# A hybrid decoder layer on one core: products stored early are written into PSUM, the opening norms move, factors load further ahead

## The chip, the core and the metric

The kernel runs on one core of one Trainium2 chip. The metric is the device time of one execution in microseconds (us). TensorE (PE) does matrix products into PSUM; VectorE (DVE) and ScalarE (ACT) work on SBUF and PSUM; GpSimd (POOL) and SyncE (SP) mostly start DMAs here. Each engine runs its own instructions in the order they were written out for it, and an instruction that waits on a semaphore holds up all that stand behind it on that engine. The same is true of the DMA starts on the SP, ACT and POOL queues.

The order on each engine is not written by hand. A planner works from the program's order, in which every instruction gets a priority by its place; a block marked `high_priority(offset=n)` is treated as if it stood n instructions earlier. `self.lead` is 300, `self.urgent` is 1000. The order is fixed when the program is built.

## The reference, cut to what matters

One decoder layer over 1024 tokens of width 1024 (float32): a SwiGLU half-step, a mixer (recurrence, sliding-window attention, attention into a memory of 256 tokens, merged by gates), a second SwiGLU half-step.

```python
def rms_norm(x, g):
    y = xf * lax.rsqrt(jnp.mean(xf * xf, axis=-1, keepdims=True) + NORM_EPS)
    return (y * g.astype(jnp.float32)).astype(x.dtype)

def swiglu(u, w_in, w_out):
    gate, up = jnp.split(u @ w_in, 2, axis=-1)
    return (jax.nn.silu(gate) * up) @ w_out

f1 = swiglu(rms_norm(h, ffn1_pre_g[l]), ffn1_w_in[l], ffn1_w_out[l])
h = h + HALF_STEP * rms_norm(f1, ffn1_post_g[l])
...
mem_n = rms_norm(mem, mem_norm_g[l])
km, vm = jnp.split(mem_n @ w_kv, 2, axis=-1)
...
f2 = swiglu(rms_norm(h, ffn2_pre_g[l]), ffn2_w_in[l], ffn2_w_out[l])
h = h + HALF_STEP * rms_norm(f2, ffn2_post_g[l])
```

## The kernel before, in words

Activations lie with features on the 128 partitions and tokens along the free dimension, in two halves of 512 tokens (h0, h1). A weight block of 128 by 512 is loaded as a "raw" on SP's queue (`raw`, L136), cast by ACT to a high part `w_hi` (L154) and subtracted by DVE to a low part `w_lo` (L156); a product is then three matmuls per block of 128 (high by high, high by low, low by high, L247 to L249), so `product` (L257) is 12 matmuls and `project` 24 for each half of the tokens. Up to eight such weight operands are prepared ahead (`OPS`), and up to four raws.

**The first half-step's input** (`ffn_in`, L480) multiplies by Winograd's variant of Strassen's scheme: seven products in place of eight, over the quarters x11, x21 (h0) and x12, x22 (h1). For each of 22 column blocks the gate part needs only b11 and b21, which are x11 and x21 after the norm; the rest needs factors that mix both halves of the tokens. The gate part of the first 16 blocks (`FIRST`; 14 in the second half-step) is done ahead. Its first product `m` and the finished gate `g` are stored to DRAM (`first_d`, on POOL's queue) and loaded again by `ffn_in_pair` (L515), which does the remaining five products of such a "rest" block (60 matmuls). The other blocks, "pairs", do all seven products in one go.

- **Opening** (`unscaled_gates`, L411): the first `UNSCALED` = 6 gate blocks are multiplied before the norm's factor is known, with x times the gain split into high and low parts. The sum of squares of h0 goes through PE (`rstd`, L268: 8 small matmuls, some 13 small DVE instructions, 4 small matmuls that spread the result), with blocks 2 and 3 multiplied between. Blocks 0 to 3 are scaled on DVE (L439, L440), h0 is normed (`factors_norm`, L358, 8 DVE instructions), split (`factors_first`, L360: 8 casts on ACT, 8 subtractions on DVE at L304), and blocks 4 and 5 are scaled as they leave PSUM (L426). Then blocks 6 and 7 are multiplied with the normed h0 (`gates_ahead`, L475). The norm of h1 has blocks 8 and 9 between; `factors_part` and `factors_end` then make the mixed factors, and blocks 10 to 15 follow.
- **A rest block** (L515): the stored `m1` is added by DVE to two results as they leave PSUM (L533) and a third time at the end (L564). Pair blocks do the same two evictions as ACT copies (L535). The bank `px` takes the products with t2, t3 and t4 in turn; `pz` those with t1 and b22. `up` (L546) must have read `px` before the product with t4 may write on.

PSUM has eight banks of 128 by 512: four for tiles tagged "mm" (`px`, `py`, `po`, `pq`, `pgate` and others) and four for "bg" (`pz`, `pu`, the small norm results).

**The half-step's output** (`ffn_outs`, L615) runs seven phases of 11 steps; a step is 48 matmuls onto four banks. In each step a weight operand and a "hidden" factor from DRAM are used. `out_hidden` (L581) loads the factor on SP's queue into `hid` (3 buffers), casts on ACT (L303) and subtracts on DVE (L304) into two of the 32 `u` tiles; `out_next` (L590) keeps `OUT_AHEAD` = 6 of them written ahead in the program, with priority `lead`. In the first half-step the order of phases is a11, s1, s2, s3, s4, a22, a12. Phase s2 adds onto a11's banks; ACT then copies these four banks (L611, `urgent`) and s3 adds onto the same banks.

**The mixer's memory part** (`memory_kv`, L1061): after the memory's norm, with `GATES_MEM` = 4 gate blocks of the mixer between, PE makes four key products into `pq` banks, DVE scales each out of PSUM (L1074, normal priority) and ACT's queue stores it (L1075); two value products follow into two more `pq` banks. At that time DVE runs the 62 steps of `rwkv_invert` (L896, L897), a serial chain that stands earlier in the program.

## Time and profile before

| | us |
|---|---|
| median of 3 runs | 2371.98 |
| lowest and highest | 2368.95, 2372.22 |
| the profiled execution's own time | 2373.79 |
| its span, first to last instruction | 2372.1 |
| DVE busy (share of the span) | 1657.1 (70%) |
| ACT busy | 971.1 (41%) |
| POOL busy | 234.4 (10%) |
| TensorE's mean granted clock | 0.989 |

How to read it: an engine's busy time is averaged over stages that differ. What counts at a place is which wait ends last there. The stages in the profiled execution, by the lines that PE works on: the opening to about 112 us, rest blocks to about 330, pair blocks to about 450, the first output half to about 690, the mixer to about 1680, the second half-step's input to about 2140, its output to the end.

### The profile page before, as it was taken

What the parts mean: (1) busy time and instruction counts of PE and PEld (TensorE: products, weight loads), DVE (VectorE), ACT (ScalarE), POOL (GpSimd) and SP (SyncE); (2) the same over time, 40 slices, a digit from 0 to 9 for tenths busy, and PEclk for the clock granted to TensorE, in tenths of its full rate; (3) what the DMA queues carried; (4) which work ended last, traced back from release to release, by engine and by line L of the source; (5) the groups of instructions that cost most, each with busy time, mean ns of one, the idle gap of its engine ahead of it and who ended that gap; (6) DMA issues with size and microseconds to landing.
All of it is one profiled execution on the core that took longest, in us unless ns stands there. A gap on an engine that the chain in (4) does not pass through costs nothing.

```text
span 2372.1 us, 34157 instructions
## 1 busy us (share of the span) xinstructions
PE 2308.0 (97%) x12204; PEld 1874.0 (79%) x12204; DVE 1657.1 (70%) x2720; ACT 971.1 (41%) x1828; POOL 234.4 (10%) x365
## 2 busy tenths in 40 slices
PE   8999999999999999999999999999999999999997
PEld 6877888787877778877776887778888888887886
DVE  7887876676787767992445357765897787667765
ACT  7522223444445443222335355524563223344551
POOL 1111111100000000011220000042011111100000
PEclk9999999999999999999999999999999999999998
DMA  6555542677632426244335434364465543338753
GB/s 236 196 182 171 178 148 97 219 245 248 221 125 85 160 103 208 94 159 154 119 105 174 147 110 156 112 208 152 159 230 173 201 169 133 107 132 295 254 203 107
DMA packets 221386, 395.69 MB, mean 167 GB/s; under 512 B 39680, under 2 KB 67840, under 8 KB 220960
## 3 DMA queue, kind: packets, MB, share of 16 engines
q1 hardware_dynamic: 187488, 308.75, 39.4%
q0 software_dynamic: 17120, 56.11, 6.4%
q10 hardware_dynamic: 16608, 28.65, 3.5%
q8 instruction: 96, 1.57, 0.3%
q14 instruction: 74, 0.61, 0.1%
HBM read 281.74 MB, written 110.62 MB: 165 GB/s over the span
## 4 chain that ended last, share of the span: by engine, by line
PE 75%; DVE 12%; DMA 6%; issue 3%; ACT 3%; SPq 0%; DVEq 0%; ACTq 0%
PE px L248 7%; PE px L249 7%; PE px L247 7%; PE pgate L247 3%; PE pgate L249 3%; PE pz L247 3%; PE pz L248 3%; PE pz L249 3%; PE pgate L248 3%; PE po L247 2%; PE po L248 2%; PE po L249 2%; PE pu L248 2%; PE pu L247 2%; PE pu L249 2%
## 5 line engine op out<-in xcount | busy, mean ns | idle before, releaser
L154 ACT CAST w_hi<-w_raw 128x512 fp32r<-128x512 f32 x566 | 349.6, 620 | 822.4 <-PE px L248 192.9
L156 DVE TENSOR_TENSOR w_lo<-w_raw,w_hi 128x512 fp32r<-128x512 f32 x558 | 394.4, 709 | 209.2 <-ACT w_hi L154 203.0
L247 PE MATMUL pgate<-u,w_hi 128*128 128x512 f32 x384 | 154.5, 402 | 0.0
L247 PE MATMUL po<-u,w_hi 128*128 128x512 f32 (+1 forms) x396 | 146.0, 369 | 8.6 <-ACT acc L611 4.9
L249 PE MATMUL pgate<-u,w_lo 128*128 128x512 f32 x384 | 153.8, 400 | 0.0
L248 PE MATMUL pgate<-u,w_hi 128*128 128x512 f32 x384 | 153.0, 398 | 0.0
L248 PE MATMUL px<-u,w_hi 128*128 128x512 f32 x376 | 147.7, 394 | 4.3 <-DVE u L304 4.2
L247 PE MATMUL px<-u,w_hi 128*128 128x512 f32 x376 | 146.6, 392 | 3.7 <-ACT u L421 2.6
L249 PE MATMUL px<-u,w_lo 128*128 128x512 f32 x376 | 147.1, 392 | 0.2 <-DVE w_lo L156 0.2
L248 PE MATMUL po<-u,w_hi 128*128 128x512 f32 (+1 forms) x396 | 145.3, 367 | 0.0
L249 PE MATMUL po<-u,w_lo 128*128 128x512 f32 (+1 forms) x396 | 145.3, 367 | 0.0
L247 PE MATMUL px<-f,w_hi 128*128 128x512 f32 x352 | 138.6, 394 | 4.6 <-DVE up L546 2.3
L247 PE MATMUL pz<-u,w_hi 128*128 128x512 f32 x352 | 137.6, 391 | 1.0 <-DVE m L533 0.8
L248 PE MATMUL px<-f,w_hi 128*128 128x512 f32 x352 | 138.2, 393 | 0.0
L249 PE MATMUL px<-f,w_lo 128*128 128x512 f32 x352 | 138.1, 392 | 0.0
L249 PE MATMUL pz<-u,w_lo 128*128 128x512 f32 x352 | 137.0, 389 | 0.0
L248 PE MATMUL pz<-u,w_hi 128*128 128x512 f32 x352 | 137.0, 389 | 0.0
L303 ACT CAST u<-hid 128x512 fp32r<-128x512 f32 x154 | 95.3, 620 | 95.2 <-DMA hid<-fact_d 94.0
L304 DVE TENSOR_TENSOR u<-hid,u 128x512 fp32r<-128x512 f32 x154 | 105.2, 686 | 31.4 <-ACT u L303 30.6
L552 POOL DMA_DIRECT2D fact_d<-g x88 | 47.5, 540 | 575.3 <-DVE g L551 268.0
L249 PE MATMUL pu<-u,w_lo 128*128 128x512 f32 x264 | 102.7, 389 | 0.0
L248 PE MATMUL pu<-u,w_hi 128*128 128x512 f32 x264 | 102.7, 389 | 0.0
(368 smaller groups left out, 5396.6 us busy)
## 6 DMA issues: line engine op xcount, KB each, us to landing
w_raw<-in_ffn_in SPq DMA_DIRECT2D x236, 256.0 KB
w_raw<-in_ffn_out SPq DMA_DIRECT2D x198, 256.0 KB
hid<-fact_d SPq DMA_DIRECT2D x154, 256.0 KB
w_raw<-in_win SPq DMA_DIRECT2D x112, 256.0 KB
fact_d<-g POOLq DMA_DIRECT2D x88, 256.0 KB, 2.7
fact_d<-h POOLq DMA_DIRECT2D x66, 256.0 KB, 3.8
gate_d<-gate SPq DMA_DIRECT2D x24, 512.0 KB
pk_d<-pk ACTq DMA_DIRECT2D x4, 2560.0 KB
```

Of the source, the lines that this page charges most:

```text
L154: self.nc.scalar.copy(hi, x)
L156: (engine or self.nc.vector).tensor_tensor(lo, x, hi.bitcast(F32), ALU.subtract)
L247: mm(out, wh, xh, start=first, stop=False, **kw)
L248: mm(out, wh, xl, start=False, stop=False, **kw)
L249: mm(out, wl, xh, start=False, stop=last, **kw)
L303: self.nc.scalar.copy(hi, x)
L304: self.nc.vector.tensor_tensor(lo, x, hi.bitcast(F32), ALU.subtract)
L552: store = lambda n, t: nc.gpsimd.dma_start(fact_d[FACTORS.index(n), j // 2], t)
```

## The change

Five edits:

1. **A rest block's stored product goes into PSUM.** ACT copies `m1` into the bank `px` (priority `lead`), and the product with t2 accumulates onto it. The two evictions are then ACT copies as in a pair block, and DVE's three additions of `m1` are gone. It holds for the 16 rest blocks of the first and the 14 of the second half-step.
2. **Eight unscaled gate blocks.** Blocks 6 and 7 are now multiplied with the raw x and scaled as they leave PSUM. They stand between the two parts of h1's norm. `factors_norm` for h1 is given the finished factor. Scaled gate blocks 8 to 15 all come after `factors_end` in the program.
3. **`OUT_AHEAD` is 12.**
4. **`GATES_MEM` is 6**: six of the mixer's gate blocks between the parts of the memory's norm.
5. **The keys' scaling has priority `lead`, and their store is on SP's queue.**

```diff
-OUT_AHEAD = 6
+OUT_AHEAD = 12
-UNSCALED = 6
+UNSCALED = 8
-GATES_MEM = 4
+GATES_MEM = 6
@@ def unscaled_gates
+        pair = lambda j, evict=None, between=None: self.gate_pair(f, j, lower, upper, pool, m_tile, evict, between)
+
+        def scaled(j):
+            for i, (m, g) in enumerate(pair(j, scale)):
+                self.store_first(first_d, j + i, m, g, g)
+
         self.prefetch()
         split(range(KH))
-        done = []
-        done += self.gate_pair(f, 0, lower, upper, pool, m_tile, between=lambda: split(range(KH, KD)))
-        sq = self.sum_squares([t[0] for t in x], pool)
-        ps = self.rstd([sq], D, pool, between=lambda: done.extend(self.gate_pair(f, 2, lower, upper, pool, m_tile)))
+        done = pair(0, between=lambda: split(range(KH, KD)))
+        sq = [self.sum_squares([t[0] for t in x], pool)]
+        ps = self.rstd(sq, D, pool, between=lambda: done.extend(pair(2)))
...
+        sq = [self.sum_squares([t[1] for t in x], pool)]
         self.factors_norm(x, HALVES[0], f + "_pre_g", pool, rs)
         self.factors_first(x)
-        for j in range(4, UNSCALED, 2):
-            for i, (m, g) in enumerate(self.gate_pair(f, j, lower, upper, pool, m_tile, scale)):
-                self.store_first(first_d, j + i, m, g, g)
+        scaled(4)
+        self.opening_rs = self.rstd(sq, D, pool, between=lambda: scaled(6))
@@ def ffn_in
             ahead = iter(range(UNSCALED if pre else 0, FIRST[f], 2))
-            between = lambda: self.gates_ahead(f, next(ahead), pool, first_d)
             if pre:
                 pre(pool)
-                between()
             self.factors_begin(pool)
             for part in parts:
-                norm(part, pool, between)
+                norm(part, pool)
@@ def ffn_in_pair
             nc.sync.dma_start(m1, first_d[j, 0])
             nc.sync.dma_start(g0, first_d[j, 1])
+            with self.tc.high_priority(offset=self.lead):
+                nc.scalar.copy(px, m1)
...
             with self.tc.high_priority(offset=self.lead):
-                if ahead:
-                    V.tensor_tensor(t, ps, m1, ALU.add)
-                else:
-                    nc.scalar.copy(t, ps)
+                nc.scalar.copy(t, ps)
...
-        self.product(px, self.take(name, j), fs["t2"], ahead)
+        self.product(px, self.take(name, j), fs["t2"])
...
-        if ahead:
-            V.tensor_tensor(m1, m1, px, ALU.add)
-            V.tensor_tensor(g0, g0, m1, ALU.mult)
-        else:
-            V.tensor_tensor(g0, g0, px, ALU.mult)
+        V.tensor_tensor(g0, g0, px, ALU.mult)
@@ def memory_kv
-            V.tensor_tensor(t, ps[:, :MEM], rs, ALU.mult)
-            nc.scalar.dma_start(km_d[:, h], t)
+            with self.tc.high_priority(offset=self.lead):
+                V.tensor_tensor(t, ps[:, :MEM], rs, ALU.mult)
+            nc.sync.dma_start(km_d[:, h], t)
@@ def build
-                            lambda part, pool, between: self.factors_norm(x, part, "ffn1_pre_g", pool, between=between),
+                            lambda part, pool: self.factors_norm(x, part, "ffn1_pre_g", pool, self.opening_rs),
```

## The prediction

> **What bounds the kernel now.** First the page: engines, clock, chain.

> ```profile
> PE 2308.0 (97%) x12204; PEld 1874.0 (79%) x12204; DVE 1657.1 (70%) x2720; ACT 971.1 (41%) x1828; POOL 234.4 (10%) x365
> ...
> PEclk9999999999999999999999999999999999999998
> ...
> PE 75%; DVE 12%; DMA 6%; issue 3%; ACT 3%; SPq 0%; DVEq 0%; ACTq 0%
> ```

> PE is busy for 97% of the span. The change removes no matmul, so it can only win PE's 64 us of idle time and what the clock loses behind it. Next, PE's waits (total, times, longest, in us):

> ```profile
> PE po L247 <- ACT acc L611: 4.9, 1, 4.9
> ...
> PE px L248 <- DVE u L304: 4.2, 1, 4.2
> PE pq L247 <- DVE km L1074: 3.9, 2, 3.2
> PE po L247 <- DVE g L567: 3.6, 2, 1.9
> ...
> PE px L247 <- DVE up L546: 2.3, 1, 2.3
> PE px L247 <- ACT w_hi L154: 2.3, 1, 2.3
> ...
> PE px L247 <- ACT u L303: 1.0, 1, 1.0
> ```

> Five places, each touched by an edit. Their full price is read from windows around them: stretch, its length, PE busy and number of matmuls, then PEld, DVE, ACT, POOL, granted clock, DMA.

> ```profile
> 44.00:58.00 14.00, 8.76 (x28) 6.26 (x27) 12.03 (x20) 7.54 (x13) 1.87 (x4) 0.76 0.44 166
> 146.00:156.00 10.00, 7.71 (x28) 5.89 (x27) 6.83 (x11) 2.39 (x4) 0.00 (x0) 0.83 0.45 156
> 205.00:215.00 10.00, 7.72 (x28) 5.94 (x27) 6.58 (x11) 2.39 (x4) 0.00 (x0) 0.83 0.31 114
> 453.00:458.00 5.00, 3.09 (x14) 2.27 (x13) 4.37 (x8) 2.01 (x4) 1.99 (x4) 1.00 0.92 303
> 541.00:553.00 12.00, 7.09 (x25) 5.42 (x25) 7.66 (x13) 6.69 (x13) 0.00 (x0) 0.86 0.81 264
> 1038.00:1052.00 14.00, 10.15 (x37) 7.78 (x37) 13.86 (x20) 4.38 (x8) 4.95 (x3) 0.76 0.51 168
> ...
> 300.00:440.00 140.00, 140.00 (x619) 115.97 (x618) 93.97 (x147) 51.01 (x86) 15.12 (x28) 1.00 0.36 125
> ```

> The last row is the undisturbed pace: 140 / 619 = 0.226 us a matmul. A window's loss is its length less its matmuls times 0.226, plus some 0.3 for a matmul or two counted over its edges. **Opening** (44:58): 14 - 28 x 0.226 + 0.3 = 8.0 us. **Rest blocks** (146:156, 205:215): 10 - 6.3 + 0.3 = 4.0 each. **First output step** (453:458): 2.1. **Phase s2 to s3** (541:553): 12 - 5.7 + 0.3 = 6.6. **Memory keys** (1038:1052): 14 - 8.4 + 0.3 = 5.9. Together 30.6 us. Each loss but one is larger than its idle time, because the granted clock falls too: the rest-block stalls idle 2.3 us, and a share of 0.83 over 10 us is another 1.7.

> [...]

> **The change part by part.**

> *Opening: eight unscaled blocks.* PE waits for the first factors of the normed h0. On DVE (start, length, line):

> ```profile
> 46.46 4.06 DVE L358 SCALAR_TENSOR_TENSOR acc<-acc,vecs,u 128x512 f32<-128x512 f32 x6
> 50.44 0.68 DVE L304 TENSOR_TENSOR u<-acc,u 128x512 fp32r<-128x512 f32 x1
> ...
> 64.89 0.16 DVE L280 TENSOR_SCALAR rsm<-ps_ms 128x4 f32<-128x4 f32 x1 [2.38 <-PE ps_ms L275]
> ...
> 67.61 0.16 DVE L291 SCALAR_TENSOR_TENSOR rsy<-rsq,rsy 128x4 f32<-128x4 f32 x1
> ```

> The norm ends at 50.5 and the first subtraction at 51.1; PE had idled 1.0 + 4.2 us by then and run four matmuls, so it had wanted block 6 at about 45. With blocks 6 and 7 unscaled, PE has 48 more matmuls (10.9 us) that need neither, plus the 12 small ones of h1's norm, moved here from between later blocks; it asks for the factors at about 57. DVE gains, ahead of them, the small chain of h1's norm (64.89 to 67.77: 2.9 us) and up to four scalings of 0.6 us, which `urgent` puts first: 50.5 becomes about 56, so the first factor lands just as it is asked for, the later ones at one per 1.2 us against one per 0.7 wanted, but b21 only 5.4 us later. I leave 0.5 us: **-7.5**. Four scalings (2.4 us of DVE) are new; they lie under PE. h1's factor is known at 57 instead of 76 (its sum at 64.9 and two blocks, 10.9 us), so DVE starts on the mixed factors 19 us earlier, while PE comes to the rest blocks only 8 us earlier. POOL's queue has as many stores as before. Bounds: nothing won, 8.0 won.

> *Rest blocks.* Removed on DVE, for each of 30 blocks, two L533 and one L564; added on ACT, two copies like L535 and one from SBUF into PSUM.

> ```profile
> L533 DVE TENSOR_TENSOR u<-px,m 128x512 f32<-128x512 f32 x30 | 20.6, 687 | 2.3 <-PE px L249 0.9
> L564 DVE TENSOR_TENSOR m<-m,px 128x512 f32<-128x512 f32 x30 | 20.5, 682 | 4.3 <-PE px L249 3.8
> ...
> L535 ACT COPY u<-px 128x512 f32<-128x512 f32 x14 | 8.1, 581 | 0.0
> ...
> L154 ACT CAST w_hi<-w_raw 128x512 fp32r<-128x512 f32 x566 | 349.6, 620 | 822.4 <-PE px L248 192.9
> ```

> DVE loses 3 x 20.6 = 62 us, ACT gains 30 x (2 x 0.58 + c). No row shows ACT writing PSUM; the nearest are 0.58 (out of PSUM) and 0.62 (within SBUF); I take 0.62 for c, some 53 us in all. [...]

> None of this is PE's time in itself. What it buys is the stall at 148 (DVE's own rows):

> ```profile
> 148.25 0.69 DVE L179 TENSOR_TENSOR w_sum<-w_raw 128x512 f32<-128x512 f32 x1 [3.35 <-DMA w_raw<-in_ffn_in]
> 148.98 0.69 DVE L180 TENSOR_TENSOR w_raw<-w_raw 128x512 f32<-128x512 f32 x1
> 149.59 0.68 DVE L546 TENSOR_TENSOR up<-px,m 128x512 f32<-128x512 f32 x1
> ```

> `up`, for which PE waits, stands behind a weight sum that waits 3.35 us for its raw. The raw was late because raw buffers come free when DVE has made `w_lo`, and DVE is nearly full here. Stage by stage (first rest blocks, pair blocks, second rest blocks):

> ```profile
> 112.00:330.00 218.00, 212.88 (x920) 174.10 (x920) 178.11 (x281) 58.25 (x95) 27.54 (x51) 0.98 0.52 176
> 330.00:434.00 104.00, 104.00 (x461) 86.14 (x460) 65.31 (x101) 38.99 (x67) 10.79 (x20) 1.00 0.28 99
> 1790.00:1980.00 190.00, 189.54 (x834) 155.74 (x833) 151.59 (x239) 52.13 (x84) 24.91 (x47) 1.00 0.52 176
> ```

> DVE goes from 178 to 178 - 16 x 2.06 = 145 of 218 us (67%), ACT from 58 to 86 (40%). The pair blocks, which evict by ACT already, run at 63% and 37% without one stall: the nearest row says that both go, **-8.0**. Also `m1` (two buffers) now comes free when it is copied, not at the block's end, so SP's load of the next no longer holds raws behind it. The new wait is that of the product with t2 for the copy; behind the copy on ACT stand weight casts. `px` has four banks in turn and the copy has priority `lead`, so it may run as soon as the bank of four blocks before is free, three blocks ahead of its use: nothing, and if that cover is gone, one load and one copy a block. In the second half-step there is next to nothing to win (834 matmuls in 190 us). Bounds: two stalls won; or stalls added on ACT's queue (rivals).

> *Factors 12 steps ahead.* ACT at the end of s2, and the count of factor casts since 430:

> ```profile
> 546.79 0.62 ACT L303 CAST u<-hid 128x512 fp32r<-128x512 f32 x1 [1.76 <-DMA hid<-fact_d]
> 547.32 1.55 ACT L611 COPY acc<-po 128x512 f32<-128x512 f32 x3
> ```

> ```profile
> 430.00:547.00 117.00, 29.43 (x48) 1.00 0.77 253
> ```

> The copies for which PE waits 4.9 us stand behind a cast that waits for its factor's DMA. But 48 casts at step 33 is 15 steps ahead already: priority `lead` runs them as far as 32 `u` tiles (16 factors) allow. So the edit only reorders SP's queue: factors go ahead of raws, and the DMA engines stay as full. Earlier factors mean a shorter wait for that cast; later raws may put a weight cast in its place. Ends: 6.6 won, or lost once more; I take half, **-3.3**. At the first output step (2.1, and its twin in the second half-step) the same factors were already ahead: **0**, ends -4 and +4.

> *Memory keys.* DVE's and ACT's rows:

> ```profile
> 1039.16 0.42 DVE L1074 TENSOR_TENSOR km<-pq,mem_rs 128x256 f32<-128x256 f32 x1
> ```

> ```profile
> 1040.03 1.82 ACT L154 CAST w_hi<-w_raw 128x512 fp32r<-128x512 f32 x3 [8.95 <-DVE km L1074]
> ```

> The first scaling runs behind the serial inversion; ACT's queue, held by its store, cannot cast the value weights for 9 us, and the banks stay taken. With priority `lead` the four scalings (0.42 us each) go between the inversion's steps, as `w_lo` does, and no cast stands behind a store. The stores now stand on SP's queue before raws; a scaling on time makes that free, and eight operands are ready if not. Two more gate blocks (96 matmuls, 21.7 us) before the keys are taken off those behind. The inversion's end slips by under 2 us under gate blocks. **-5.9**; ends 0 and 5.9.

> Sum: 7.5 + 8.0 + 3.3 + 5.9 = 24.7. The profiled execution took 2373.8, 1.8 above the median of the runs: 2373.8 - 24.7 = 2349.1, less 1.8: **2347**.

> **The rivals.** *The depth does nothing* (the edit doesn't do what it says): 15 steps were ahead before, so the s2 stall stays. 2347 + 3.3 = 2350.

> *Rest stalls stay*, on the other engine: the copies of `px` and `pz` stand on ACT behind weight casts, and these wait:

> ```profile
> ACT w_hi L154 <- DVE w_raw L181: 125.9, 35, 7.8
> ```

> 35 waits of 3.6 us on average, up to 7.8. For it: PE gives a copy only 12 matmuls (2.7 us). Against it: the pair blocks have these rows too. Two such stalls: 2347 + 8 = 2355.

> *The opening's wait comes back* at block 8, DVE being late by what it gained (5.3 us) and more: 2355.

> *No change*: the last three together, 2347 + 3.3 + 8 + 7.5 = 2366, within 0.2%.

> *Slower*: ACT's queue holds the copies up in many of the 30 rest blocks, 4.0 us each. With the other gains kept (16.7) and the two old stalls gone, it decides from seven blocks on; at twelve it gives 2347 + 48 = 2395. For it: in-order ACT, 35 waits. Against it: the order is laid out with the casts' waits in view, and the second half-step's 14 blocks show no such stall on a fuller DVE.

> **How the numbers follow.** Forecast (all four gains, s2 half to wholly won, 2343 to 2349): 0.34. Depth does nothing: 0.24. Rest stalls stay: 0.16. Opening's wait comes back: 0.10. No change: 0.08. Slower: 0.08. The range leaves out the slower rival and most of no change, and adds 4 below the forecast's end for the first output steps and 9 above 2355 for two rivals at once: 2339 to 2364. Faster by over 0.2% (below 2367.2; about what a measurement can tell from no change): 0.84; same 0.08; slower 0.08.

> **What would show it.** Right: PE's waits without `u` L304, `up` L546, `km` L1074; rest blocks starting some 8 us earlier; DVE busy near 1600, ACT near 1024; clock 1.00 in 100 to 330. Wrong: PE waits on `px` for ACT's copies (at L535 or the new copy), L611 still 4.9, block 8 waiting for L304.

## The result and the profile after

| | median us | runs | lowest to highest |
|---|---|---|---|
| before | 2370.89 | 4 | 2368.95 to 2372.22 |
| changed | 2348.42 | 4 | 2343.42 to 2350.74 |

The changed kernel takes 0.9903 of the time before (95% interval 0.9884 to 0.9922): 22.5 us less. The prediction was 2347. The profiled execution of the changed kernel is the fastest of its four, 2343.42 us (span 2341.7), and lies 30.4 us below the profiled one of before, which at 2373.79 took longer than each of the four runs in the table. Where the difference between 30.4 and 22.5 comes from is taken up under the sum below.

The page of the changed kernel: engines, granted clock in 40 slices, chain.

```profile
PE 2296.0 (98%) x12204; PEld 1867.8 (80%) x12204; DVE 1606.0 (69%) x2634; ACT 1017.3 (43%) x1916; POOL 233.5 (10%) x365
...
PEclk9999999999999999999999999999999999999998
...
PE 88%; DVE 6%; DMA 2%; ACT 2%; issue 1%; SPq 0%; DVEq 0%; ACTq 0%
```

The matmuls are the same 12204. DVE lost 51 us of work, ACT gained 46, and the chain that ended last runs through PE for 88% of the span in place of 75%. PE's waits in this execution (total, times, longest):

```profile
PE ptr L1182 <- DVE sc L1172: 5.8, 5, 2.7
PE ps_ms L275 <- DVE sq L317: 5.0, 6, 2.0
PE po L247 <- DVE g L565: 3.9, 2, 2.2
...
PE px L247 <- DVE up L548: 0.6, 1, 0.6
```

The rows for `u` L304 at `px`, `km`, the copies `acc` and the cast `w_hi` are gone; what is left at the top belongs to the attention and the norms, and to the first output step. Windows at the former places (the opening; s2 to s3; the memory keys; the first output step; columns as in the prediction):

```profile
44.00:58.00 14.00, 14.00 (x72) 11.63 (x70) 12.97 (x33) 7.01 (x14) 2.86 (x6) 1.00 0.77 263
525.00:537.00 12.00, 12.00 (x54) 9.93 (x54) 8.70 (x14) 7.30 (x14) 0.00 (x0) 1.00 0.73 236
1036.00:1050.00 14.00, 14.00 (x67) 11.47 (x66) 4.87 (x8) 5.59 (x9) 6.99 (x7) 1.00 0.81 266
430.00:444.00 14.00, 11.23 (x41) 8.83 (x42) 11.30 (x19) 7.30 (x13) 2.71 (x5) 0.88 0.82 273
```

Three of the four are full at a clock of 1.00; the first output step now loses more than before, because 0.88 of the clock was granted. The rest stage, from the first product with t1 to the first pair block, before and after:

```profile
112.00:339.40 227.40, 222.28 (x962) 181.86 (x962) 184.50 (x292) 60.75 (x100) 28.98 (x54) 0.98 0.52 174
```

```profile
103.30:321.00 217.70, 217.70 (x961) 180.11 (x961) 154.02 (x239) 82.87 (x141) 29.57 (x55) 1.00 0.53 177
```

The same 960 matmuls without one idle moment, and 30 us less on DVE. Stage by stage, each measured between the first matmuls of neighbouring stages:

| stage | before | changed | difference |
|---|---|---|---|
| start to the first product | 9.0 | 8.4 | -0.6 |
| opening, to the first rest block | 103.0 | 94.9 | -8.1 |
| rest blocks | 227.3 | 217.7 | -9.7 |
| pair blocks | 111.5 | 112.4 | +0.9 |
| first output phase | 32.1 | 34.0 | +1.9 |
| s2 and s3, to s4 | 66.4 | 59.8 | -6.5 |
| mixer: small products before the gates, to the gram products (with the keys) | 352.6 | 344.4 | -8.2 |
| everything else together | | | -0.1 |

### The profile page after: what moved, and what is told of

Its sections match the earlier page's. It is cut to its first block, busy times and chain, and to the rows that moved or that the text cites. A ratio compares the mean times of both kernels' runs of the same rounds, so it can differ in the third digit from the quotient of the medians.

```text
span 2341.7 us, 34138 instructions
## 1 busy us (share of the span) xinstructions
PE 2296.0 (98%) x12204; PEld 1867.8 (80%) x12204; DVE 1606.0 (69%) x2634; ACT 1017.3 (43%) x1916; POOL 233.5 (10%) x365
## 4 chain that ended last, share of the span: by engine, by line
PE 88%; DVE 6%; DMA 2%; ACT 2%; issue 1%; SPq 0%; DVEq 0%; ACTq 0%
PE px L248 8%; PE px L247 8%; PE px L249 7%; PE pgate L247 4%; PE pgate L249 4%; PE pgate L248 3%; PE pz L248 3%; PE pz L249 3%; PE pz L247 3%; PE po L247 3%; PE po L248 3%; PE po L249 3%; PE pu L248 2%; PE pu L247 2%; PE pu L249 2%; PE pq L249 2%
## 5 line engine op out<-in xcount | busy, mean ns | idle before, releaser
L154 ACT CAST w_hi<-w_raw 128x512 fp32r<-128x512 f32 x566 | 350.0, 620 | 733.4 <-PE px L248 192.6
L247 PE MATMUL pgate<-u,w_hi 128*128 128x512 f32 x384 | 154.3, 402 | 0.0
L249 PE MATMUL pgate<-u,w_lo 128*128 128x512 f32 x384 | 153.8, 400 | 0.0
L248 PE MATMUL pgate<-u,w_hi 128*128 128x512 f32 x384 | 153.0, 398 | 0.0
L247 PE MATMUL px<-u,w_hi 128*128 128x512 f32 x384 | 149.2, 390 | 1.1 <-ACT u L421 1.1
L247 PE MATMUL po<-u,w_hi 128*128 128x512 f32 (+1 forms) x396 | 145.9, 369 | 4.1 <-DVE g L565 3.9
L248 PE MATMUL px<-u,w_hi 128*128 128x512 f32 x384 | 149.3, 391 | 0.1
L249 PE MATMUL px<-u,w_lo 128*128 128x512 f32 x384 | 149.3, 390 | 0.0
L248 PE MATMUL po<-u,w_hi 128*128 128x512 f32 (+1 forms) x396 | 145.5, 368 | 0.0
L249 PE MATMUL po<-u,w_lo 128*128 128x512 f32 (+1 forms) x396 | 145.4, 367 | 0.0
L247 PE MATMUL px<-f,w_hi 128*128 128x512 f32 x352 | 137.3, 390 | 0.6 <-DVE up L548 0.6
L248 PE MATMUL px<-f,w_hi 128*128 128x512 f32 x352 | 137.0, 389 | 0.0
L249 PE MATMUL px<-f,w_lo 128*128 128x512 f32 x352 | 137.0, 389 | 0.0
L249 PE MATMUL pz<-u,w_lo 128*128 128x512 f32 x352 | 136.9, 389 | 0.0
L247 PE MATMUL pz<-u,w_hi 128*128 128x512 f32 x352 | 136.9, 389 | 0.0
L248 PE MATMUL pz<-u,w_hi 128*128 128x512 f32 x352 | 136.9, 389 | 0.0
L303 ACT CAST u<-hid 128x512 fp32r<-128x512 f32 x154 | 95.4, 619 | 85.5 <-DMA hid<-fact_d 81.9
L304 DVE TENSOR_TENSOR u<-hid,u 128x512 fp32r<-128x512 f32 x154 | 105.3, 687 | 27.9 <-ACT u L303 27.2
L247 PE MATMUL pu<-u,w_hi 128*128 128x512 f32 x264 | 102.9, 390 | 0.0
L249 PE MATMUL pu<-u,w_lo 128*128 128x512 f32 x264 | 102.7, 389 | 0.0
```

What stands on the lines that cost most here:

```text
L154: self.nc.scalar.copy(hi, x)
L247: mm(out, wh, xh, start=first, stop=False, **kw)
L248: mm(out, wh, xl, start=False, stop=False, **kw)
L249: mm(out, wl, xh, start=False, stop=last, **kw)
L303: self.nc.scalar.copy(hi, x)
L304: self.nc.vector.tensor_tensor(lo, x, hi.bitcast(F32), ALU.subtract)
```

## The experiments

They ran in three groups, each on a chip of its own beside runs of the kernel before; a ratio is always to the runs of before in its own group (medians 2371.33, 2369.74 and 2369.86).

### Undoing one edit at a time

**The depth set back.**

```diff
-OUT_AHEAD = 12
+OUT_AHEAD = 6
```

> The changed kernel with the depth of the factor loads set back from 12 to 6 steps; the other edits stay. Theory A (the depth removed the stall between s2 and s3, because factors go ahead of raws on SP's queue): PE again waits some 4.9 us for the copies of the accumulators (the row acc, 4.9, 1, 4.9 of the kernel before), s3 starts 6.6 us later against s2 than in the changed kernel, and the whole is some 6 us (0.25%) above it, near 2355. Theory B (the depth does nothing, since priority had 15 steps ahead already; the stall went because the earlier edits moved the stages by 15 us against the DMA traffic): no wait for acc over 1 us, s2 and s3 as long as in the changed kernel, time the same within its 7 us of spread.

Measured: 2349.62 us, ratio 0.9912 (0.9895 to 0.9928), hardly above the changed kernel. Its profile has the wait, but a shorter one:

```profile
PE po L247 <- ACT acc L609: 2.6, 1, 2.6
```

s2 and s3 took 62.7 us against 59.8 and no half clock followed (1.00 granted from 530.7 to 545.7). Between the two theories: the wait is back, its price is half of what theory A had. One profile doesn't settle it, though: the repeat of the changed kernel further down has such a wait with twelve steps as well.

**DVE adds the stored product again** (edit 1 undone).

```diff
-            with self.tc.high_priority(offset=self.lead):
-                nc.scalar.copy(px, m1)
...
-                nc.scalar.copy(t, ps)
+                if ahead:
+                    V.tensor_tensor(t, ps, m1, ALU.add)
+                else:
+                    nc.scalar.copy(t, ps)
...
-        self.product(px, self.take(name, j), fs["t2"])
+        self.product(px, self.take(name, j), fs["t2"], ahead)
...
-        V.tensor_tensor(g0, g0, px, ALU.mult)
+        if ahead:
+            V.tensor_tensor(m1, m1, px, ALU.add)
+            V.tensor_tensor(g0, g0, m1, ALU.mult)
+        else:
+            V.tensor_tensor(g0, g0, px, ALU.mult)
```

> The changed kernel with the stored products again added by VectorE and not written into PSUM; the other edits stay. Theory A (the relief of VectorE removed the two stalls of the first rest blocks): one or two waits of PE for up or u of some 2.3 us come back between 105 and 325, the granted clock there falls below 1.00, the rest stage is 8 to 10 us longer, the whole near 2356, VectorE's busy time 62 us higher. Theory B (the stalls went because the opening now gives VectorE a later start of demand, or because raw loads fall otherwise): VectorE's busy time rises by 62 us but the rest stage keeps its length within 1 us, and the time is that of the changed kernel.

Measured: 2349.75 us, ratio 0.9912 (0.9895 to 0.9928). The rest stage took 218.8 us, 1.1 more than with the edit, its clock was 1.00, and neither wait for `up` came back. Theory A fell: with the other edits in place, the relief of DVE isn't needed to keep these stalls away.

**The opening of before** (edit 2 undone: six unscaled blocks, h1's norm after the factors of h0).

```diff
-UNSCALED = 8
+UNSCALED = 6
```

(with `unscaled_gates`, `ffn_in` and `factors_norm` as before)

> The changed kernel with the opening of the kernel before: six unscaled blocks, the norm of the second half of the columns after the factors; the other edits stay. Theory A (the two more unscaled blocks cover the wait for the first factors): PE waits for u again, 4.2 us and the half clock behind it, the rest blocks start 8 us later than in the changed kernel (at 111 to 112 us), the later stages keep their lengths, the whole is 8 us above. Theory B (the opening's 8 us are partly given back or the rest stage's gain hangs on the earlier factors): the rest stage gets longer as well, by one or two stalls of 4 us each, 12 to 16 us above the changed kernel in all.

Measured: 2355.33 us, ratio 0.9932 (0.9915 to 0.9949), about 7 us above the changed kernel. The opening took 102.9 us, with the 4.2 us wait for `u`; the rest stage stayed at 218.3. Theory A held. Together with the run before this one, either of the two edits can be taken away and the rest stage stays whole.

**The keys at plain priority** (edit 5 undone; six gate blocks stay).

```diff
-            with self.tc.high_priority(offset=self.lead):
-                V.tensor_tensor(t, ps[:, :MEM], rs, ALU.mult)
-            nc.sync.dma_start(km_d[:, h], t)
+            V.tensor_tensor(t, ps[:, :MEM], rs, ALU.mult)
+            nc.scalar.dma_start(km_d[:, h], t)
```

> The changed kernel with the scaling of the memory keys at plain priority again and their stores on ScalarE's queue; six gate blocks still stand ahead of the keys. Theory A (priority and queue removed the stall): PE waits for km again, some 3 to 4 us, and the keys' stage is 6 to 8 us longer than in the changed kernel. Theory B (the two gate blocks moved ahead of the keys give the serial inversion 22 us more, and that alone was enough): no wait for km, keys' stage as in the changed kernel within 1 us.

Measured: 2345.39 us, ratio 0.9896 (0.9880 to 0.9913). No wait for `km`; from the small products to the gram products 344.5 us, as with the priority. Theory B held. DVE's rows of this kernel show why:

```profile
1030.04 0.28 DVE L895 TENSOR_TENSOR inv<-inv,itmp 128x62 f32<-128x62 f32 x1
1030.23 0.68 DVE L156 TENSOR_TENSOR w_lo<-w_raw,w_hi 128x512 fp32r<-128x512 f32 x1
1030.83 0.42 DVE L1072 TENSOR_TENSOR km<-pq,mem_rs 128x256 f32<-128x256 f32 x1
```

The last step of the inversion (62 wide) is over before the first scaling is due, so there is nothing left to be put ahead of. The time is no longer than that of the changed kernel, so edit 5 buys nothing that can be told.

### One edit alone, and the rest of the keys

**Edit 1 alone on the kernel before** (the diff of the second experiment the other way round).

> The kernel before with the stored products written into PSUM, nothing else. The undone versions left the rest stage without stalls whether this edit or the opening was taken back. Theory A (either edit alone is enough): VectorE's busy time in the rest stage falls from 184 to some 158 us, both waits for up (2.3 us each) go, the stage from the first product with t1 to the first pair block takes 218 to 219 us (227.3 before), the time is 8 to 9 us under the kernel before, near 2363. Theory B (the earlier undone version lost its stalls by accident of the order, and this edit does nothing): one or both waits stay, and the time is that of the kernel before.

Measured: 2365.60 us, ratio 0.9979 (0.9967 to 0.9991): 4.1 us, half of theory A's 8 to 9. Its waits are gone as theory A has it; PE has no wait in its rest stage:

```profile
113.00:330.60 217.60, 217.60 (x962) 180.19 (x961) 158.16 (x245) 84.32 (x145) 29.50 (x55) 1.00 0.53 181
```

**Edit 2 alone on the kernel before.**

> The kernel before with eight unscaled blocks and the earlier second norm, nothing else. Theory A (the opening alone removes the rest stalls too, since the mixed factors are made earlier against PE and VectorE's queue is ahead when the rest blocks begin): PE's wait for u (4.2) and both waits for up go, opening 8 us and rest stage 8 to 9 us shorter, 16 us under the kernel before, near 2355. Theory B (each edit removes its own stall): opening 8 us shorter, rest stage still 227 us, near 2363.

Measured: 2358.65 us, ratio 0.9952 (0.9938 to 0.9965): 11.1 us, where theory A had 16. The opening is 8.2 shorter, and the rest stage, with DVE as full as ever, has no wait either:

```profile
103.30:322.40 219.10, 219.03 (x961) 179.61 (x960) 180.53 (x285) 59.98 (x97) 28.88 (x54) 1.00 0.54 178
```

So each edit alone is enough. All profiles bear this out: the rest stage took 223.0, 223.8 and 227.3 us in the three with neither edit (a wait of over 2 us in each), 217.6 and 218.3 with edit 1 alone, 218.8 and 219.1 with edit 2 alone, 217.7 to 219.2 in the seven with both, and in these eleven no wait is longer than 0.5 us. That the other executions with neither edit took 223 us also means that some 5 us were to be won here, and not the 8 to 9 that the theories' times count on.

The two edits don't do the same thing, though. The view of the tile `up` in the rest stage lists for what DVE sat idle before it (total, times). With edit 2 alone, and then in the changed kernel:

```profile
L549 DVE TENSOR_TENSOR up<-px,m x16: 682/683/692, 109.4 to 314.5; 128x512 f32<-128x512 f32 x16
...
  PE px L249: 1.4, 1
```

```profile
L548 DVE TENSOR_TENSOR up<-px,m x16: 683/691/692, 109.1 to 313.1; 128x512 f32<-128x512 f32 x16
...
  PE px L249: 11.3, 11
```

In the changed kernel DVE is ready and waits for PE in 11 of 16 blocks; with edit 2 alone in one. From the end of `up` to the product with t4 that needs it there were 1.76 us in the usual case with edit 1 (10 or 11 of 16 blocks in these profiles) and some 0.5 without. With edit 2 DVE starts its last subtraction for the mixed factors 3.6 us before the rest stage begins; in the kernel before, and with edit 1 alone, it starts it 2.3 us after. That these 6 us are what makes edit 2 enough fits the traces, but no run changed them alone.

**Four gate blocks ahead of the keys** (edit 4 undone, priority kept).

```diff
-GATES_MEM = 6
+GATES_MEM = 4
```

> The changed kernel with four gate blocks ahead of the memory keys and not six; the keys' priority and their stores on SyncE's queue stay. Theory A (either edit is enough): no wait for km; from lora to the gram products as in the changed kernel, 344 us within 1 us; time the same. Theory B (the 22 us of gate blocks were the whole cause, priority nothing): PE waits for km again, 3 to 4 us and the half clock, stage 6 to 8 us longer.

Measured: 2352.44 us, ratio 0.9931 (0.9915 to 0.9946), above the changed kernel by 4.0 us in the medians and by some 6 in the ratios (0.9903, and 0.9907 in its repeat); the stage took 349.8 us. PE's wait:

```profile
PE pq L247 <- DVE km L1073: 3.2, 2, 2.1
```

DVE's rows, with the keys' first product begun at 1004.9:

```profile
1013.17 1.85 DVE L895 TENSOR_TENSOR inv<-inv,itmp 128x686 f32<-128x686 f32 x1
1015.05 0.84 DVE L894 TENSOR_TENSOR itmp<-inv 128x650 f32<-128x650 f32 x1
1015.80 0.68 DVE L156 TENSOR_TENSOR w_lo<-w_raw,w_hi 128x512 fp32r<-128x512 f32 x1
1016.40 0.83 DVE L895 TENSOR_TENSOR inv<-inv,itmp 128x650 f32<-128x650 f32 x1
1017.15 0.42 DVE L1073 TENSOR_TENSOR km<-pq,mem_rs 128x256 f32<-128x256 f32 x1
```

The priority does put the scalings between the inversion's steps, but the first of them only at 1017, 12 us after the keys began. Theory B held in the main: the stage is 5.3 us longer, a little under its 6 to 8, and the two gate blocks do nearly all of it.

**Six gate blocks alone on the kernel before.**

```diff
-GATES_MEM = 4
+GATES_MEM = 6
```

> The kernel before with six gate blocks ahead of the memory keys in place of four; priority and queue of the scalings as before. Theory A (the two gate blocks alone removed the stall, as taking back the priority suggests): no wait for km, from lora to the gram products 344 to 346 us in place of 352.6, clock 1.00 at 1020 to 1070, time 6 to 8 us under the kernel before, near 2362. Theory B (they only did so together): the wait for km stays at 2 us or more.

Measured: 2363.18 us, ratio 0.9968 (0.9956 to 0.9980): 6.7 us. No wait for `km`; the stage took 347.9 us against 352.6. Theory A held, with a stage 2 us longer than it had: 3.4 us at half clock stand in it at 756, far ahead of the keys (1.7 us of time). The profile of before has the like at 759, the changed kernel's has none.

**The depth alone on the kernel before.**

```diff
-OUT_AHEAD = 6
+OUT_AHEAD = 12
```

> The kernel before with factors loaded 12 steps ahead and nothing else. Theory A (the depth itself removes the wait for the accumulators' copies): the wait of 4.9 us falls under 1 us, from s2 to s4 60 to 61 us in place of 66.4, time 5 to 6 us under the kernel before, near 2364. Theory B (the depth helps only with the earlier rest stages): wait 2.5 to 5 us, 63 to 66 us, time within 3 us of the kernel before.

Measured: 2369.54 us, ratio 0.9994 (0.9984 to 1.0004): no difference that can be told. Its profiled execution was the fastest of the 12, 2362.89, and has no wait for `acc` (59.8 us from s2 to s4). The profile speaks for theory A and the times for B: the depth does not act in every execution. The same profile shows that the rest stalls vary too. The code of this stage is that of before, yet PE waits for `up` once:

```profile
PE px L247 <- DVE up L546: 2.2, 1, 2.2
```

Its rest stage took 223.1 us and that of the run with six gate blocks alone 223.8, against the 227.3 of the execution that the prediction had read.

### The changed kernel once more

> The changed kernel once more, unaltered, to see what differs between its own runs (2343.4 to 2350.7 so far, the profiled one the lowest). Theory A (the runs differ by how many of their short idle times are followed by 3.4 us of half clock, 1.7 us each, and by waits whose cause is a DMA's arrival): the stages before 430 and the keys' stage repeat within 1.7 us, the waits for u, for km and for acc over 1 us stay away, and the sum of the half-clock stretches accounts for most of the difference in time. Theory B (the 22.5 us of the medians and the 30.4 of the profiled runs differ because one of the four stalls is back in other runs): a second profile shows one of these waits again. Median near 2348.

Measured: 2347.94 us, ratio 0.9907 (0.9893 to 0.9920), profiled at 2347.94. Theory B held here: one of the four stalls is back.

```profile
PE po L247 <- ACT acc L609: 3.6, 1, 3.6
```

ACT's rows at the end of s2, in this execution and in the first one of the same kernel:

```profile
525.09 0.62 ACT L303 CAST u<-hid 128x512 fp32r<-128x512 f32 x1 [1.65 <-DMA hid<-fact_d]
525.61 0.61 ACT L154 CAST w_hi<-w_raw 128x512 fp32r<-128x512 f32 x1
527.98 0.62 ACT L303 CAST u<-hid 128x512 fp32r<-128x512 f32 x1 [1.75 <-DMA hid<-fact_d]
528.51 1.55 ACT L609 COPY acc<-po 128x512 f32<-128x512 f32 x3
```

```profile
524.62 0.62 ACT L154 CAST w_hi<-w_raw 128x512 fp32r<-128x512 f32 x1 [1.57 <-issue]
525.14 0.62 ACT L303 CAST u<-hid 128x512 fp32r<-128x512 f32 x1
525.67 1.76 ACT L609 COPY acc<-po 128x512 f32<-128x512 f32 x3
```

The order is the same: a factor's cast, then the copies. In the first execution the factor lies there; in the second ACT waits for its transfer, and the copies wait behind it. From the first matmul of s2, 46 casts had begun after 27 us in the second execution, 47 in the first, 45 in the kernel before. This count sorts all 14 profiles: in the seven with 47 the wait is 0.9 us at most, in the seven with 45 or 46 it is 2.4 to 4.9. All five with six steps ahead are of the second kind, and two of the nine with twelve. Over all profiles, s2 and s3 took 62.7 to 66.5 us with six steps ahead (five profiles, mean 64.7, a wait in each) and 59.8 to 65.3 with twelve (nine profiles, mean 61.2, five without any wait, two under 1 us, two of 2.4 and 3.6).

Theory A fell: both executions have three stretches of 3.4 us at half clock ahead of the span's last one, so these explain nothing of the 4.5 us between them; s2 and s3 alone are 5.5 us longer in the second.

### A version that beats both

The first output step waits for the last pair block's product with the gate. DVE's rows of the changed kernel, and PE's row that waits:

```profile
437.95 0.68 DVE L562 TENSOR_TENSOR h<-g 128x512 f32<-128x512 f32 x1
438.55 0.68 DVE L304 TENSOR_TENSOR u<-hid,u 128x512 fp32r<-128x512 f32 x1
439.15 0.68 DVE L565 TENSOR_TENSOR g<-g,px 128x512 f32<-128x512 f32 x1
```

```profile
439.88 0.61 PE L247 MATMUL po<-u,w_hi 128*128 128x512 f32 x1 [2.20 <-DVE g L565]
```

The bank `px` was complete at 433.6; the product that frees it ran at 439.2, behind factor work with priority. First, that priority for all blocks:

```diff
-        V.tensor_tensor(g0, g0, px, ALU.mult)
+        with self.tc.high_priority(offset=self.lead):
+            V.tensor_tensor(g0, g0, px, ALU.mult)
```

> The changed kernel with the last product of each rest and pair block, the gate's times px, at the priority of the other evictions. In the changed kernel PE's only long wait in the feed-forward parts is for this product at the first output step (3.9 us in two waits, the first with 3.4 us of half clock behind it), and it starts at 439.2 although px was complete at 433.7. Theory A (it stands behind factor work on VectorE by its priority alone): no wait of po for g over 0.3 us, clock 1.00 at 430 to 450, 3 to 6 us under the changed kernel, near 2344. Theory B (VectorE is too full there and something else comes late, a weight part or a factor): the wait changes its name and the time stays.

Measured: 2345.08 us, ratio 0.9898 (0.9882 to 0.9913). Theory A held: the wait is gone at both output starts, the first output phase took 29.9 us against 34.0, and the time is 3.3 us below the median of the changed kernel. In the second half-step's rest blocks a wait for `up` of 1.9 us stood. Then for the last block alone:

```diff
-        V.tensor_tensor(g0, g0, px, ALU.mult)
+        with self.tc.high_priority(offset=self.lead if j == KF - 1 else 0):
+            V.tensor_tensor(g0, g0, px, ALU.mult)
```

> The changed kernel with the priority of the last product raised in the last pair block alone, since raising it in all blocks took both waits at the first output steps away, but a wait of 1.9 us for up stood in the second half-step's rest blocks. Theory A (the priority of 43 other products caused that wait): no wait of po for g over 0.3 us, no wait for up over 1 us, 2 to 4 us under the changed kernel of the same chip, near 2344. Theory B (that wait was the arrival of a raw and belongs to the run): no different from the version with all blocks.

Measured: 2343.21 us, ratio 0.9884 (0.9867 to 0.9900); its four runs lie between 2341.94 and 2344.51, all below the five of the changed kernel in the same group (2346.17 to 2351.64). The window of the first output step:

```profile
430.00:444.00 14.00, 14.00 (x63) 11.58 (x63) 10.96 (x19) 6.67 (x12) 2.69 (x5) 1.00 0.88 284
```

A wait for `up` of 2.2 us stands in this profile as well, so it isn't the priority of the other blocks that causes it: theory B for that part. DVE's rows before it:

```profile
1800.32 0.69 DVE L179 TENSOR_TENSOR w_sum<-w_raw 128x512 f32<-128x512 f32 x1 [5.12 <-DMA w_raw<-in_ffn_in]
1803.59 0.68 DVE L548 TENSOR_TENSOR up<-px,m 128x512 f32<-128x512 f32 x1
```

DVE isn't full here (busy for 25.9 of the 44 us from 1766 to 1810): it had been idle for 5.12 us when the raw came, and `up` stands behind the raw's work. A wait for `up` of over 1 us stands in the second half-step's rest blocks of five of the nine profiles with edit 1 (three of them without any priority on the last product), and in none of the five without it. There edit 1 buys nothing: the stage took 192.1 us on average without it and 192.3 with it. Why the raw comes late there was not looked into by a run.

About 4.7 us are won in all (2347.94 less 2343.21).

## Why the prediction was right, point by point

The median came out 1.4 us above the forecast. The mechanism of the sum was right: PE's four stalls with the clock behind them; but two terms were credited to the wrong edit or to one edit alone, and the sizes hold only as means over executions.

**Opening, -7.5.** Measured -8.1 in the profile, and about 7 us in time when the edit was taken back. The step was right: the first subtraction for a factor of h0 ends at 56.2 (about 56 in the prediction), and PE, which begins block 8 at 57.9 (about 57), waits nowhere for L304 at `px`; the rest blocks begin 8.7 us earlier.

**Rest blocks, -8.0.** -9.7 between the two profiled executions. The step that failed is the one that gave the gain to edit 1 alone: "What it buys is the stall at 148". It buys it, but edit 2 alone buys it too. The prediction had the clue in its own working: "DVE starts on the mixed factors 19 us earlier, while PE comes to the rest blocks only 8 us earlier", and did not carry it on to a stall at which `up` is late on DVE (that this lead is the reason fits the traces and is not shown). The reason that it gave for the late raw, that DVE is nearly full, can hardly be it in the second half-step, where the raw came late with DVE busy for 59% of the time. The size was also read from an execution with two stalls; two others of the same code had one, so the mean of the three profiles is 224.7 us, 7 above the 217.7 of the changed kernel. That 8.0 came out between 7.0 and 9.7 owes something to luck. The prices of the parts were near: the copy into PSUM took 0.59 us for the estimated 0.62, the time of a cast within SBUF.

```profile
L530 ACT COPY px<-m 128x512 f32<-128x512 f32 x30 | 17.7, 591 | 8.1 <-DVE g L565 6.5 <-DMA m<-first_d 0.8 <-DMA w_raw<-in_ffn_in 0.6
```

DVE's total fell to 1606.0 and ACT's rose to 1017.3, where near 1600 and near 1024 stood. The durations of all DVE instructions add up to 60 us less and those of ACT to 52 more, near the forecast's 62 and 53; the page's busy time, in which what overlaps counts once (rows listed at 0.68 us start some 0.60 apart), changed by 51 and 46.

**s2 to s3, -3.3.** Half of 6.6 was taken for want of a reason for either end. The means over profiles differ by 3.5 (64.7 to 61.2), so the number fits by luck, and not because half of the wait goes: in most executions it goes whole, in others it stays. Timed alone the edit gave 0.3 us less, its interval -3.8 to +0.9; what it is worth alone stays open within that. The argument that it only reorders SP's queue fits both: one factor more or less cast by then goes with the wait in all 14 profiles. Why it comes in time in most executions with twelve steps and not in all stays open. (A step of the output is 12 matmuls, 132 in a phase of 29.9 us, and not 48 as the description of the kernel has it.)

**Memory keys, -5.9.** -8.2 in the profile, of which 1.7 is the half clock at 759 that has nothing to do with the keys, so some 6.5; 6.7 timed alone for edit 4 (4.7 to 10.4). The step that failed: "With priority `lead` the four scalings ... go between the inversion's steps". They do, but too late: without the two gate blocks PE still waits 3.2 us in all, of 3.9 in before. The two gate blocks, 21.7 us of PE work, which the prediction counted as moved and without effect of their own, let the inversion end before the keys need DVE.

**First output step, 0 (±4).** +1.9 in the profile, +0.1 in the repeat; PE's idle time there is of like length in all (1.9 us in before, 2.2 in the changed kernel, 2.0 in its repeat), and it is the clock granted behind it that differs (0.50 for 3.4 us in the changed kernel; 1.00 in the two others).

**The sum.** Taken as means, 8.1 + 7.0 + 3.5 + 6.7 = 25.3 are won, near the predicted 24.7 and the measured 22.5. The 30.4 between the profiled executions is a good run against a poor one. Against the means over profiles the rest blocks of before stand 2.6 us high, and s2 and s3 1.7 high in before and 1.4 low in the changed kernel. Half-clock stretches without the one in which the span ends add up to 37.5 us in before and 10.2 in the changed kernel; 23.9 of the 37.5 belong to the stalls and are in their prices, and the other 13.7 against 10.2 are 1.7 us of time. Together, as an estimate, that is 7.4 of the 7.9 us.

**The rivals.** PE waited nowhere for ACT's copies of `px` or `pz`, so neither "rest stalls stay" nor "slower" came. The opening's wait did not come back at block 8. "The depth does nothing" is the one that partly did: its time, 2350, is about as near to the measured one as the forecast's.

## What to carry to other kernels

A stall of about 2 us on a full engine may be removed by either of two edits, here by less work on that engine or by an edit with which it began its backlog earlier; undo each edit before crediting it, for the sum can be right while the credit is wrong. Raising an instruction's priority helped only where its place in the order of its engine moved far enough: with four gate blocks PE still waited 3.2 us for `km`. Giving PE other work until a serial chain is over was worth more here (6.7 us). Read a stall from several executions before pricing it, when what ends it is a transfer.

## What the runs showed of the hardware

```profile
436.70:440.11 3.41, 1.21 (x6) 0.71 (x5) 3.37 (x6) 1.14 (x3) 0.80 (x2) 1.00 0.93 324
440.11:443.53 3.42, 3.42 (x9) 2.66 (x9) 1.96 (x4) 1.61 (x3) 1.08 (x2) 0.50 1.02 317
```

In the kernel before 1.9 us at the same place were followed by full clock:

```profile
455.16:458.57 3.41, 1.52 (x7) 1.27 (x8) 3.03 (x6) 0.62 (x1) 1.16 (x3) 1.00 0.97 335
458.57:462.00 3.43, 3.43 (x17) 2.83 (x16) 1.67 (x3) 2.19 (x4) 2.08 (x6) 1.00 0.86 320
```

Counted over the cells at full clock of all 14 profiles, without the start and the end of the span (matmul ends are modelled, so the bounds are rough): with over 1.95 us of idle time the next cell was at half clock in 41 of 41, with 1.7 to 1.95 in 23 of 37, with 1.4 to 1.7 in 3 of 39, with less in none of 9292. In the profiles of before and of the changed kernel alone it is 9 of 9, 3 of 7, none of 4 and none of 1315. Where the grid cuts a wait can be seen in the changed kernel: the 2.2 us above lay in one cell and cost another 1.7 (3.42 us at 0.50), while a longer wait, 2.7 us from 1431.7, lay over two cells, with 1.75 us in the first, and cost no clock:

```profile
1429.99:1433.41 3.42, 1.67 (x8) 1.05 (x6) 1.16 (x5) 2.33 (x9) 0.00 (x0) 1.00 0.70 243
1433.41:1436.82 3.41, 2.49 (x20) 1.96 (x22) 3.22 (x10) 1.82 (x4) 0.00 (x0) 1.00 0.53 154
```

Idle times of over 2 us stand three times in the changed kernel's profile and seven times in that of before, without the start. A wait that falls into one cell in one run and over two in another would be a source of the spread between runs of one kernel (7 us in the changed kernel's first group), but it isn't shown as one: the two profiled executions of the changed kernel have equally many such cells.
